# Outer products of a gated recurrence: from a broadcast through DRAM to masked matmuls on TensorE

## The chip, the cores and the metric

The kernel runs on one NeuronCore of a Trainium2 chip, in one launch. The metric is the device time of one execution in microseconds (us); less is better. Engines are named as in the profile: PE (TensorE) with its weight loads PEld, DVE (VectorE), ACT (ScalarE), POOL (GpSimd) and SP (SyncE, which only issues transfers here).

## What is computed

One decoder layer runs on 512 prompt tokens and, beside them, on one new token of each of 8 sample requests: a mixer of two head groups (a gated linear recurrence, HGRN2, and differential attention), memory cross-attention and a SwiGLU block. The sample's attention reads a paged cache of 4096 keys and values per request (64 MiB each).

The change is in the sample's recurrence. For each request b and each of 4 heads h, with a state S of 128 x 128:

```
S_new[b,h] = f[b,h][:, None] * S[b,h] + k[b,h][:, None] * v[b,h][None, :]
o[b,h]     = S_new[b,h].T @ q[b,h]
```

S_new is an output too (8 requests x 256 KB).

## The kernel before

**Staging.** The prompt's products are split in two fp32r parts (hi and lo for weights, sh and sl for activations), so each tile of a weight costs three PE matmuls of 128 x 512 (tiles `mm`). Weights stream from DRAM through `raw` tiles; ACT rounds them to `hi`, DVE forms the remainder `lo`, both at most HILO = 3 steps ahead of PE. The weight order is: input projection, memory keys and values (w_mk, w_mv), w_out, w_mq, w_mo, then the feed-forward chunks. The paged keys (`cache_k`) and then the values (`cache_v`) stream through six 512 KB buffers (`stream`, lines 934 to 940; KBUFS) on SP's queue while the prompt's products run; `score_keys` (line 991) makes the `ks` matmuls from them. SP issues a load when a buffer has come free.

**What sets the order.** Every piece of work is a generator, and a planner written in the kernel (`Weave`, line 312) picks, while the program is built, which generator goes on. It uses a clock of its own (`Clock`, line 134) with costs per instruction and per transfer (all transfers priced by bytes alone, line 257, in one line behind each other), and a rank per generator. So the order of instructions on each engine is fixed before the run, and each engine takes its instructions strictly in that order. The sample's recurrence has rank 4, the prompt's attention heads rank 3, the prompt's products rank 9 (they fill what is left). Tiles of PSUM are eight banks of 128 x 512 fp32; a generator asks for one (`at_room`) and gives it back (`at_give`), at most AT_MAX = 4 of the kind `at`.

**The recurrence** (`sample_recurrence`, line 1474). It starts when the input projection of the sample is done. skT holds the keys as [128 key components, head, request], sfT the gates, svq the values as [4 heads x 32 rows, 128], of which 8 rows per head are requests. svq is written to DRAM (`spill`, line 569, tile `vd`). Then for each request b in turn: POOL issues the load of the state (`st`, 256 KB, line 1492) and a load of that request's four value rows from DRAM to all 128 partitions (`load_row`, line 575: tile `kv`, 256 KB, line 1494); ACT scales the four heads of `kv` by the key column (line 1498), which makes the outer products in place; DVE masks the queries (`qm`) and makes st = f * st + kv, one instruction per head (line 1509); POOL issues the store of the new state (line 1513); PE makes the outputs (`so`, line 1517) and DVE adds them up in `ohg`. One request's transfers are issued only after the store of the one before.

**What follows.** The end of the recurrence (`S["hgo"]`, line 1533, after the transposition of `on`) is asked for at line 2152: if it is there before the third step of w_out's weights, the sample's half of the output projection is made from the weights as they pass for the prompt (lines 2153 to 2163), and four of eight extra loads of w_out (line 1879) drop out; otherwise all eight are loaded later.

All instructions are recorded through one helper, so the profile shows L305 for each; they are told apart by the names of their tiles.

Of the kernel before, what the change touches and what calls it, by code (L numbers as in the profile page):

```python
# [12 lines left out]
F32 = mybir.dt.float32  # L13
F32R = mybir.dt.float32r
I32 = mybir.dt.int32
AF = mybir.ActivationFunctionType
ALU = mybir.AluOpType
AX = mybir.AxisListType
PSUM = bass.MemoryType.PSUM

P = 128
# [4 lines left out]
NB = 8  # L26
HEADS = 4
# [351 lines left out]
def decode_step(ctx: ExitStack, tc: tile.TileContext, io: dict):  # L379
# [4 lines left out]
    act = clock.engine("act", real.scalar)  # L384
    dve = clock.engine("dve", real.vector)
    pool = clock.engine("pool", real.gpsimd)
# [8 lines left out]
    dp = ctx.enter_context(tc.tile_pool(name="dp", bufs=1, space=bass.MemoryType.DRAM))  # L395
    cnt = [0]

    def nm(s):
        cnt[0] += 1
        return f"{s}{cnt[0]}"  # L400

    def ring(p, shape, tag, bufs, name, dt=F32):
        return clock.alloc(tag, bufs, p.tile(list(shape), dt, tag=tag, bufs=bufs, name=nm(name)))

    def keep(shape, name):
        return cp.tile(list(shape), F32, name=name)


    def slot(s, shape=(P, T), dt=F32):
        return fp.tile(list(shape), dt, tag="slot", bufs=SLOTS, name=nm(s))  # L410
# [18 lines left out]
    def bank_counter(kind, most):  # L429
        banks[kind] = 0  # L430

        def room(n=1):
            fits = lambda: banks[kind] + n <= most and sum(banks.values()) + n <= 8
            yield fits
            yield clock.bank_free(n)
            while not fits():
                yield fits
            banks[kind] += n

        def give(n=1):  # L440
            banks[kind] -= n
            clock.release(kind, n)

        def tile(s=kind):
            return clock.bank(kind, ps.tile([P, T], F32, tag="ps", bufs=8, name=nm(s)))

        return room, give, tile

    mm_room, mm_give, mmt = bank_counter("mm", MM_MAX)
    at_room, at_give, att = bank_counter("at", AT_MAX)  # L450
# [5 lines left out]
    def small(shape, s="s", st="p", bufs=3):  # L456
        n = int(np.prod(shape[1:]))
        return ring(sp, shape, f"{st}{n}", bufs, s)
# [4 lines left out]
    def rsmall(shape, s):  # L463
        return small(shape, s, "r", 2)

    def quadt(s, shape=(P, P), tag="quad", bufs=4):
        return ring(sp, shape, tag, bufs, s)
# [4 lines left out]
    def mm(out, a, b, start, stop):  # L472
        pe.matmul(out, lhsT=a, rhs=b, start=start, stop=stop)

    def tr(out, a, i):
        pe.transpose(out, a, i)
# [17 lines left out]
    for n, shape in PARAMS:  # L494
        c = int(np.prod(shape))
# [9 lines left out]
    ident, ropes, cmask = views["ident"], views["ropes"], views["cmask"]  # L505
# [54 lines left out]
    def s_tr(q, use):  # L560

        yield from at_room()
        pt = att("str")
        tr(pt[:, :P], q, ident)
        yield (pt,)
        use(pt[:, :P].rearrange("p (g b) -> p g b", b=32))
        at_give()

    def spill(q, name):

        d = dp.tile([P, P], F32, name=name)
        pool.dma_start(d, q)
        return d.rearrange("(g b) c -> b g c", b=32)

    def load_row(dst, d, b):

        pool.dma_start(dst.rearrange("p (g c) -> p g c", g=4), d[b].partition_broadcast(P))


    sizes = [512] * (DFF // 512)  # L580
# [725 lines left out]
    def sigmoid(out, e, z):  # L1306

        act.activation(e, z, AF.Exp, scale=-1.0)
        yield
        dve.tensor_scalar(out, e, BIG, 1.0, op0=ALU.min, op1=ALU.add)  # L1310
        dve.reciprocal(out, out)
# [139 lines left out]
    def s_headnorm(o, use):  # L1451

        sq = quadt("hsq")
        s1 = rsmall([P, 1], "hs1")
        act.activation(sq, o, AF.Square, accum_out=s1)
        rs = rsmall([P, 1], "hrs")
        rstd_from(s1, rs, 1.0 / P)
        yield
        on = quadt("on")
        dve.tensor_scalar(on, o, rs, None, op0=ALU.mult)  # L1460
        yield
        yield from s_tr(on, use)
# [11 lines left out]
    def sample_recurrence(sqT, sfT, svq, sgT):  # L1474
        skT = keep([P, 4, 8], "skT")
        lb3 = lb.unsqueeze(2).to_broadcast([P, 4, 8])
        om3 = omlb.unsqueeze(2).to_broadcast([P, 4, 8])
        sig = rsmall([P, 4, 8], "sig")
        yield from sigmoid(sig, skT, sfT)
        dve.scalar_tensor_tensor(skT, skT, BIG, sig, op0=ALU.min, op1=ALU.mult)  # L1480
        dve.tensor_tensor(skT, skT, om3, op=ALU.mult)
        dve.tensor_tensor(sig, sig, om3, op=ALU.mult)
        dve.tensor_tensor(sfT, sig, lb3, op=ALU.add)
        yield
        sig2 = rsmall([P, 4, 8], "sig")
        yield from sigmoid(sig2, sig2, sgT)
        dve.tensor_mul(sgT, sgT, sig2)
        vd = spill(svq, "vd")
        yield from room(2)
        for b in range(NB):  # L1490
            st = slot("st")
            pool.dma_start(st, io["state"][b])
            kv = slot("kv")
            load_row(kv, vd, b)
            yield
            for h in range(HEADS):
                sl = slice(h * P, (h + 1) * P)
                act.activation(kv[:, sl], kv[:, sl], AF.Copy, scale=skT[:, h, b : b + 1])
            qm = quadt("qm", (P, 4, 32))
            dve.tensor_tensor(  # L1500
                qm,
                sqT[:, :, b : b + 1].to_broadcast([P, 4, 32]),
                ohrow[:, 7 - b : 39 - b].unsqueeze(1).to_broadcast([P, 4, 32]),
                op=ALU.mult,
            )
            yield
            for h in range(HEADS):
                sl = slice(h * P, (h + 1) * P)
                dve.scalar_tensor_tensor(
                    st[:, sl], st[:, sl], sfT[:, h, b : b + 1], kv[:, sl], op0=ALU.mult, op1=ALU.add  # L1510
                )
            yield
            pool.dma_start(io["hg_sample"][b], st)
            yield from at_room()
            po = att("so")
            for h in range(HEADS):
                mm(po[32 * h : 32 * h + 32, :P], qm[:, h, :], st[:, h * P : (h + 1) * P], True, True)
            yield (po,)
            if b == 0:
                dve.tensor_copy(ohg, po[:, :P])  # L1520
            else:
                dve.tensor_add(ohg, ohg, po[:, :P])
            at_give()
        give(2)
        yield
        pool.memset(mixT_s[:, :4, :], 0.0)
        yield from s_headnorm(
            ohg,
            lambda oht: dve.scalar_tensor_tensor(
                mixT_s[:, :4, :8], oht[:, :, :8], hgcol, sgT, op0=ALU.mult, op1=ALU.mult  # L1530
            ),
        )
        S["hgo"] = True
# [588 lines left out]
    def follower():  # L2122
# [8 lines left out]
        for i, c0 in enumerate(ORDER):  # L2131
# [11 lines left out]
            else:  # L2143
                S["v"] = keep([P, P], "vs")
                act.copy(S["v"], out)
                weave.add(store(io["v_sample"], S["v"]), 3)
        pv_give()
        weave.add(sample_recurrence(c[0], c[512], c[1024], c[1536]), 4, "ad")
        weave.add(sample_rest(), REST)
        done["seen"] += 16  # L2150
# [462 lines left out]
```

## Time and profile before

| | |
|---|---|
| time, median of 3 runs (lowest to highest) | 1142.68 us (1138.63 to 1144.46) |
| profiled execution: its own time | 1134.85 us |
| profiled execution: span from first to last instruction | 1133.1 us |
| mean granted clock of TensorE | 0.974 of full |
| DMA traffic | 279.75 MB, mean 247 GB/s |

Times of instructions are read from the profiled execution, whose own time is 1.75 us above its span. Stretches are given in us from the start of the span. The DMA share is the mean busy share of the core's 16 DMA engines. The queue q1 carries SP's and ACT's transfers, q0 those that POOL issues. The granted clock of TensorE is given as a share of full speed, 1.00 or 0.50, and a stretch that has both shows a value in between.

### The profile page before, as it was taken

The page shows a single profiled execution, that of the slowest core. Times are in us where ns is not written, and L with a number is a line of the kernel's source. Part 1 is how long each engine was busy: PE and PEld are TensorE (multiplying, and loading weights), DVE is VectorE, ACT ScalarE, POOL GpSimd, SP SyncE. Part 2 cuts the span into 40 slices and gives each one's busy share as a digit, 9 for nine tenths or more (in the row PEclk, how much of TensorE's full clock was granted, in tenths as well). Part 3 has the DMA queues.
Part 4 walks back from the last instruction along what each step waited for, and adds up shares of the span by engine and source line. Part 5 has one row for each costly group of instructions (what it writes and reads, how often), then busy time and mean ns, then how long its engine had stood idle before and what let it go on. Part 6 is the DMA issues. An engine that isn't in the chain of part 4 may idle for free.

```text
span 1133.1 us, 23098 instructions
## 1 busy us (share of the span) xinstructions
PE 1072.3 (95%) x8846; PEld 777.3 (69%) x8846; DVE 546.1 (48%) x1126; ACT 428.3 (38%) x915; POOL 70.4 (6%) x97
## 2 busy tenths in 40 slices
PE   8999799987987889899999999999999999999997
PEld 6777587865665557466666666776577677777776
DVE  6743777534654654444443443453343333443535
ACT  6413443436454556333444332341232221222333
POOL 0000010213101110000300000000000000000002
PEclk9999899988998989999999999999999999999999
DMA  7979665998999995999998799579978982234102
GB/s 255 352 242 324 206 215 174 291 253 259 319 308 278 274 304 169 309 329 332 319 338 285 241 325 343 201 244 359 344 266 291 351 305 75 63 89 129 38 1 75
DMA packets 143376, 279.75 MB, mean 247 GB/s; under 512 B 15281, under 2 KB 20529, under 8 KB 143266
## 3 DMA queue, kind: packets, MB, share of 16 engines
q1 hardware_dynamic: 137970, 264.13, 67.8%
q0 software_dynamic: 4064, 13.05, 6.1%
q8 instruction: 69, 1.13, 0.4%
q10 hardware_dynamic: 1232, 1.11, 0.3%
q14 instruction: 41, 0.34, 0.1%
HBM read 269.35 MB, written 8.88 MB: 246 GB/s over the span
## 4 chain that ended last, share of the span: by engine, by line
PE 81%; DMA 10%; DVE 3%; issue 3%; ACT 1%; SPq 1%; POOL 0%; DVEq 0%; POOLq 0%; ACTq 0%
PE mm L305 56%; DMA cache_k<-cache_k 6%; PE pv L305 5%; PE ks L305 4%; PE sgu L305 2%; PE cs L305 2%; PE sdn L305 1%; DMA kv<-vd 1%; PE ss L305 1%; PE co L305 1%; PE sgm L305 1%; PE pd L305 1%; PE sacc L305 1%; PE oda L305 1%; PE cpv L305 1%
## 5 line engine op out<-in xcount | busy, mean ns | idle before, releaser
L305 DVE TENSOR_TENSOR lo<-raw,hi 128x512 fp32r<-128x512 f32 (+1 forms) x260 | 176.6, 681 | 434.2 <-ACT hi L305 406.1
L305 PE MATMUL mm<-sh,hi 128*128 128x512 f32 (+1 forms) x832 | 339.8, 408 | 4.2 <-ACT sh L305 3.9
L305 ACT CAST hi<-raw 128x512 fp32r<-128x512 f32 (+1 forms) x260 | 157.5, 607 | 490.5 <-PE mm L305 443.3
L305 PE MATMUL mm<-sl,hi 128*128 128x512 f32 (+1 forms) x832 | 324.1, 390 | 0.8 <-DVE sl L305 0.8
L305 PE MATMUL mm<-sh,lo 128*128 128x512 f32 (+1 forms) x832 | 323.0, 388 | 0.0
L305 PEld LDWEIGHTS mm<-sh,hi 128*128 128x128 f32 x832 | 157.2, 189 | 78.6 <-issue 39.0
L305 PEld LDWEIGHTS mm<-sh,lo 128*128 128x128 f32 x832 | 157.5, 189 | 34.0 <-DVE lo L305 0.4
L305 PEld LDWEIGHTS mm<-sl,hi 128*128 128x128 f32 x832 | 157.8, 190 | 28.9 <-DVE sl L305 1.4
L305 PE MATMUL ks<-cache_k,qst 128*32 128x128 f32 x2048 | 72.3, 285 | 16.1 <-DMA cache_k<-cache_k 16.0
L305 PEld LDWEIGHTS ks<-cache_k,qst 128*32 128x32 f32 x2048 | 57.6, 114 | 32.7 <-DMA cache_k<-cache_k 24.0
L305 PE MATMUL pv<-cache_v,wt 128*32 128x512 f32 x512 | 63.4, 608 | 0.0
L305 PE MATMUL mm<-hi,sh 128*128 128x512 f32 x128 | 54.5, 426 | 0.0
L305 PE MATMUL mm<-lo,sh 128*128 128x512 f32 x128 | 50.5, 395 | 0.0
L305 PE MATMUL mm<-hi,sl 128*128 128x512 f32 x128 | 50.5, 394 | 0.0
L305 DVE TENSOR_TENSOR res<-mm,res 128x512 f32<-128x512 f32 (+1 forms) x68 | 42.2, 652 | 9.2 <-PE mm L305 9.2
L305 PEld LDWEIGHTS pv<-cache_v,wt 128*32 128x32 f32 x512 | 14.5, 110 | 31.1 <-issue 22.1
L305 DVE SCALAR_TENSOR_TENSOR lo<-raw,par,hi 128x512 fp32r<-128x512 f32 x16 | 13.2, 826 | 35.1 <-ACT hi L305 35.1
L305 PEld LDWEIGHTS mm<-hi,sh 128*128 128x128 f32 x128 | 24.3, 190 | 7.9 <-issue 3.1
L305 PE MATMUL mm<-hi,mh 128*128 128x512 f32 x64 | 28.5, 446 | 0.9 <-ACT hi L305 0.9
L305 PEld LDWEIGHTS mm<-hi,sl 128*128 128x128 f32 x128 | 24.3, 190 | 5.5
L305 PEld LDWEIGHTS mm<-lo,sh 128*128 128x128 f32 x128 | 24.4, 191 | 4.5 <-issue 0.5
L305 PE MATMUL mm<-lo,mh 128*128 128x512 f32 x64 | 25.2, 394 | 0.2 <-DVE lo L305 0.2
(419 smaller groups left out, 1210.3 us busy)
## 6 DMA issues: line engine op xcount, KB each, us to landing
cache_k<-cache_k SPq DMA_DIRECT2D x256, 256.0 KB, 5.6
cache_v<-cache_v SPq DMA_DIRECT2D x256, 256.0 KB, 4.8
raw<-w_in SPq DMA_DIRECT2D x27, 512.0 KB, 5.1
raw<-w_down SPq DMA_DIRECT2D x22, 512.0 KB, 4.2
raw<-w_gate SPq DMA_DIRECT2D x20, 512.0 KB, 5.0
raw<-w_up SPq DMA_DIRECT2D x20, 512.0 KB, 4.5
cache_mem_k<-cache_mem_k SPq DMA_DIRECT2D x16, 512.0 KB, 6.2
cache_mem_v<-cache_mem_v SPq DMA_DIRECT2D x16, 512.0 KB, 7.4
```

Of the source, the lines that this page charges most:

```text
L305: ins = getattr(self.engine, op)(*a, **k)
```

## The change

The values are no longer written to DRAM and read back. Once, ahead of the loop, the keys are copied to a zeroed tile with 32 columns per head (`padded`), transposed on PE to rows (`krows`: row 32 h + b is the key of head h and request b), the values are laid out as a block-diagonal tile (`vcols`: rows of head h hold their value in the columns of head h, zeros elsewhere), and a mask with a column per request is made from the identity (`mine`). For each request, DVE masks the key rows (`km`), and one fp32 matmul of 128 x 128 by 128 x 512 makes all four outer products in a PSUM bank (`kv`), from which DVE's st = f * st + kv reads. The four ACT instructions and the load of `kv` are gone; the bank is held until the four DVE instructions are done.

```diff
-    def spill(q, name):
-
-        d = dp.tile([P, P], F32, name=name)
-        pool.dma_start(d, q)
-        return d.rearrange("(g b) c -> b g c", b=32)
-
-    def load_row(dst, d, b):
-
-        pool.dma_start(dst.rearrange("p (g c) -> p g c", g=4), d[b].partition_broadcast(P))
...
         dve.tensor_mul(sgT, sgT, sig2)
-        vd = spill(svq, "vd")
         yield from room(2)
+
+        krows, vcols = quadt("krows", tag="rows", bufs=1), slot("vcols")
+        pool.memset(vcols, 0.0)
+        padded, mine = quadt("padded"), rsmall([P, 32], "mine")
+        dve.memset(padded, 0.0)
+        dve.tensor_copy(padded.rearrange("p (h b) -> p h b", h=4)[:, :, :NB], skT)
+        dve.tensor_reduce(mine, ident.rearrange("p (h b) -> p b h", h=4), axis=AX.X, op=ALU.add)
+        yield
+        yield from s_tr(padded, lambda pt: dve.tensor_copy(krows, pt.rearrange("p g b -> p (g b)")))
+        for h in range(HEADS):
+            r = slice(32 * h, 32 * h + 32)
+            act.copy(vcols[r, h * P : (h + 1) * P], svq[r])
+        yield
         for b in range(NB):
             st = slot("st")
             pool.dma_start(st, io["state"][b])
-            kv = slot("kv")
-            load_row(kv, vd, b)
-            yield
-            for h in range(HEADS):
-                sl = slice(h * P, (h + 1) * P)
-                act.activation(kv[:, sl], kv[:, sl], AF.Copy, scale=skT[:, h, b : b + 1])
+            km = quadt("km")
+            dve.tensor_scalar(km, krows, mine[:, b : b + 1], None, op0=ALU.mult)
             qm = quadt("qm", (P, 4, 32))
...
             yield
+            yield from at_room()
+            kv = att("kv")
+            mm(kv, km, vcols, True, True)
+            yield (kv, st)
             for h in range(HEADS):
                 sl = slice(h * P, (h + 1) * P)
                 dve.scalar_tensor_tensor(
                     st[:, sl], st[:, sl], sfT[:, h, b : b + 1], kv[:, sl], op0=ALU.mult, op1=ALU.add
                 )
+            at_give()
             yield
             pool.dma_start(io["hg_sample"][b], st)
```

## Rows read from the trace of the kernel before

**Rows 1.** Page: busy time of the engines over the span.

```profile
PE 1072.3 (95%) x8846; PEld 777.3 (69%) x8846; DVE 546.1 (48%) x1126; ACT 428.3 (38%) x915; POOL 70.4 (6%) x97
```

**Rows 2.** Stretches: busy us of PE, PEld, DVE, ACT, POOL; clock, DMA share, GB/s.

```profile
60.00:125.00 65.00, 65.00 (x905) 51.18 (x904) 28.17 (x58) 20.18 (x47) 0.54 (x1) 1.00 0.87 291
...
212.00:415.00 203.00, 172.49 (x1716) 124.45 (x1705) 103.82 (x259) 97.07 (x243) 34.61 (x48) 0.92 0.96 281
...
450.00:600.00 150.00, 146.90 (x839) 93.80 (x838) 65.73 (x116) 59.55 (x123) 10.77 (x9) 0.99 0.94 323
...
880.00:1134.00 254.00, 242.81 (x1571) 186.64 (x1569) 108.77 (x188) 69.47 (x136) 5.75 (x6) 0.98 0.38 123
```

**Rows 3.** PE's waits in 212 to 415: total us, times, longest.

```profile
PE ks L305 <- DMA cache_k<-cache_k: 16.0, 10, 6.0
PE sc L305 <- ACT pr L305: 4.9, 1, 4.9
PE so L305 <- issue: 3.6, 1, 3.6
PE pt L305 <- ACT pr L305: 2.3, 1, 2.3
```

**Rows 4.** Stretches of 5 us with a lowered clock, columns as in rows 2.

```profile
235.00:240.00 5.00, 5.00 (x34) 3.30 (x37) 1.98 (x6) 0.58 (x1) 1.82 (x3) 0.50 0.91 315
240.00:245.00 5.00, 5.00 (x66) 4.17 (x59) 0.69 (x1) 0.62 (x1) 0.00 (x0) 0.91 1.21 104
265.00:270.00 5.00, 4.96 (x23) 2.35 (x23) 0.00 (x0) 1.47 (x3) 0.00 (x0) 0.68 0.90 289
360.00:365.00 5.00, 4.93 (x41) 2.93 (x39) 0.30 (x1) 1.16 (x5) 0.00 (x0) 0.62 1.02 367
405.00:410.00 5.00, 5.00 (x42) 3.37 (x44) 2.92 (x9) 2.92 (x8) 0.00 (x0) 0.50 0.90 311
410.00:415.00 5.00, 5.00 (x61) 3.63 (x51) 2.27 (x8) 2.88 (x7) 2.93 (x7) 0.84 0.93 281
```

**Rows 5.** ACT in 395 to 407, in order of time: start, us, what, wait.

```profile
401.97 1.28 ACT L305 ACTIVATE kv<-kv,skT 128x128 f32<-128x128 f32 x4 [9.32 <-DMA kv<-vd]
```

**Rows 6.** DMA queues in 222 to 234: packets, MB, share.

```profile
q0 software_dynamic: 83, 0.27, 47.6%
q1 hardware_dynamic: 1021, 1.92, 43.6%
```

**Rows 7.** DMA in 212 to 415: queues; issues with median us to landing.

```profile
q1 hardware_dynamic: 26544, 48.07, 67.1%
q0 software_dynamic: 2651, 8.62, 28.6%
...
st<-state POOLq DMA_DIRECT2D x8, 256.0 KB, 6.1
...
kv<-vd POOLq DMA_DIRECT2D x8, 256.0 KB, 11.4
```

**Rows 8.** PE around a 128x512 fp32 matmul and a transposition, 425 to 428.

```profile
426.47 1.02 PE L305 MATMUL ss<-hq,ones 128*128 128x512 f32 x2
427.33 0.27 PE L305 MATMUL str<-con,on 128*128 128x128 f32 x1
427.36 0.47 PE L305 MATMUL mm<-sh,hi 128*128 128x512 f32 x1
427.67 0.39 PE L305 MATMUL mm<-sl,hi 128*128 128x512 f32 x1
427.90 0.40 PE L305 MATMUL mm<-sh,lo 128*128 128x512 f32 x1
```

**Rows 9.** Groups by tile (kv, S): ns min/median/max, starts, shapes.

```profile
L305 ACT ACTIVATE kv<-kv,skT x32: 384/387/412, 232.0 to 402.9; 128x128 f32<-128x128 f32 x32
...
L305 DVE SCALAR_TENSOR_TENSOR S<-S,bhg,pst x12: 347/348/349, 147.4 to 214.5; 128x128 f32<-128x128 f32 x12
```

**Rows 10.** SP's queue: longest wait in 212 to 415.

```profile
SPq L305 <- PE ks L305: 18.6, 16, 4.6
```

## The prediction

> **What bounds the kernel now.** I read the page's busy times first: PE is busy for 95% of the span [rows 1], so over the whole kernel PE sets the pace, and a change elsewhere pays only where PE waits or runs at its lower clock. Next the stretches [rows 2]. The recurrence lies in 212 to 415. There PE is busy for 172.5 of 203.0 us, so 30.5 us are idle, the mean granted clock is 0.92, and the DMA engines are busy for 0.96 of the time. Compare two stretches that stream the same kinds of weights and cache pages: 60 to 125, with a DMA share of 0.87 and PE never idle, and 450 to 600, with 0.94 and 3.1 us idle in 150. So PE keeps up below about 0.9 and begins to lose above it; in 212 to 415 it is the transfers that are late.
>
> The waits of PE say whom it waits for [rows 3]: 16.0 us for pages of the cached keys, 4.9 and 2.3 us (sc, pt) for ACT, 3.6 us at a `so` matmul, 26.8 us together. The ACT waits come from the recurrence itself: ACT stands 9.3 us at the first `kv` scaling until the broadcast lands [rows 5], everything behind it in ACT's order stands too, and PE stops for 4.9 us. The `so` matmul comes behind the same chain. After the longer waits the clock falls to the 1.2 GHz level: with PE's busy time times one minus the granted clock, the six stretches [rows 4] cost 2.5 + 0.45 + 1.6 + 1.9 + 2.5 + 0.8 = 9.7 us.
>
> Why are the transfers late? In 222 to 234 the only transfer on POOL's queue is one `kv` broadcast: 0.27 MB take 47.6% of 12 us, 5.7 us of all 16 engines, while 1.92 MB on the other queue take 5.2 us [rows 6]. Over 212 to 415, q1 moves 48.07 MB in 67.1% of 203 us, 2.83 us per MB [rows 7]. POOL's queue has 8.62 MB in 28.6%, 58.1 us; its 6.52 MB that are not `kv` cost 18.5 us at q1's rate, which leaves 39.6 us for eight broadcasts, 5.0 each. That agrees with the 5.7 measured alone. **The broadcast takes a fifth of the stage's DMA time for a twenty-seventh of its bytes.**
>
> A rule speaks against this reading. The Trainium skill, "DMA: Bandwidth & Descriptors", section Specifications, gives 512 bytes as the least transfer for line rate, and a row of `kv` is made of 512-byte pieces: by it a broadcast would cost what its bytes cost and the change would free next to nothing. The trace disagrees (5.7 us for 0.27 MB), and I follow the trace; what would follow from the rule is the second rival.
>
> **The change, part by part.**
>
> Removed, DMA: eight broadcasts, 39.6 us of engine time (the 64 KB spill adds too little to count). The stage's DMA time was 0.96 x 203 = 194.9 us; 155.3 remain.
>
> Removed, ACT: 32 scalings of 0.387 us [rows 9], 12.4 us, and the waits ahead of them. Four small copies come instead, under 0.4 us each by the same row. ACT was busy for 97 of 203 us [rows 2], so the work was hidden; what counts is that nothing on ACT now stands behind a transfer of the recurrence.
>
> Removed, POOL: nine transfer issues; one fill of a tile is added. POOL is busy for 34.6 of 203 us: nothing, either way. The state's load and the store are issued in the same places as before.
>
> Added, PE: eight fp32 matmuls of 128x512. One such matmul (two records) took 427.33 - 426.47 = 0.86 us, and the first prompt matmul behind such a change of form started its successor after 0.31 instead of 0.23 us [rows 8]. So 8 x (0.86 + 0.08) = 7.5, and one transposition, at most 0.27: 7.8 us. PE is the engine that sets the end, so all of it counts, at full clock; at the lower level it would be up to twice that, at least 0 if it falls into a wait.
>
> Added, DVE: eight maskings of the key rows and a handful of small ones ahead of the loop, at most 0.35 us each by a three-operand instruction of 128x128 [rows 9]: under 5 us on an engine busy for 104 of 203 us. Reading `kv` from PSUM costs nothing more: that row is an instruction with a PSUM operand, and at 348 ns it has the price of the recurrence's own, which read SBUF. If DVE's cover were gone, the sum would be 5 us worse.
>
> Added, waits: `kv` needs DVE's masking and a PSUM bank, and st = f * st + kv needs the matmul and the state's load. Behind that DVE instruction stand the remainders of the weights, behind the `so` matmul the whole of PE. The state lands 6.1 us after its issue, the broadcast landed after 11.4 [rows 7], and the order of the work had room for the latter in most rounds; I take 0 for this wait, and price it as a rival. The bank is held for some 3 us a round, with prompt matmuls to run meanwhile: 0.
>
> Moved: the planner's order. Its own clock knows neither the price of the broadcast nor this stage's waits, so the places of the `so` matmuls change little; but the recurrence ends a few us earlier in it, and the transposition that ends it at 427.33 stands between the output projection's first matmuls [rows 8], right where line 2152 decides. It may fall the other way: then narrow matmuls move forward and four loads of 512 KB drop out, 2.1 MB or 5.9 us of DMA time in stretches where PE hardly waits. I take 0; what a new order can do later is bounded by the 11.2 idle us of the last stretch [rows 2], either way.
>
> **The sum.** 155.3 us of DMA for PE work of 172.5 - 9.7 + 7.8 = 170.6 us is a share of 0.91, between the two comparison stretches. I leave the idle rate of the fuller one, 3.1 / 150 x 203 = 4.2 us, to the cache: 16.0 - 4.2 = 11.8 gained. The ACT waits go (7.2), the `so` wait goes (3.6): 22.6 of 26.8. The lowered clock goes in proportion: 9.7 x 22.6 / 26.8 = 8.2. With 7.8 added: 22.6 + 8.2 - 7.8 = 23.0 us less. The profiled execution took 1134.85 us, 7.8 below the median of the runs, 1142.68; I carry the difference over and predict 1142.68 - 23.0 = 1119.7, **1120 us**. Bounds: all waits and all clock regained, 36.5 - 7.8 = 28.7 less, 1114; with the later idle time on top, 1103; without DVE's cover, with waits of 5 us left and some of the idle time added, 1130.
>
> **The rivals.**
>
> *Buffers, not bandwidth.* SP issues a page only when PE frees a buffer, and its queue waited 18.6 us for that [rows 10]. If this rather than the rate makes the pages late, the 16.0 us and their clock stay. Gained are 10.8 us of waits and the clock behind those two, 2.95 + 3.3 [rows 4]; less 7.8, that is 9.2: 1133.5. Against it: the same six buffers left no wait in 60 to 125.
>
> *The broadcast is not what fills the engines*, as the rule above would have it. Then 2.1 MB at 2.83 us per MB, 5.9 us, are saved, the stage stays at a share of 0.96, and 6 us are gained at most, with the new PE work inside the waits that remain: 1137 to 1143, no change that can be told.
>
> *A wait on the state takes the place of the wait on the values; slower.* PE takes the outer product, then `so`, in order, and a late state stops both. One such stop cost 3.65 us and 2.95 of clock [rows 3, 4], 6.6 together. The change wins 36.5 - 7.8 = 28.7 without it, so from the fifth round of eight on it is slower; in all eight rounds 52.8 stand against 28.7, 1167. Against it: the state has a 5 us shorter way than the values had [rows 7], and PE stopped so in one round of eight even then.
>
> *Given back later.* The new order loses in the last stretches what this one gains, up to the 11.2 us there and more: around 1140.
>
> **How the numbers follow.** A measurement of this kernel can tell about 0.5%, 5.7 us, from no change. Chances: the forecast 0.67 (its own range 1105 to 1131), buffers 0.12, the broadcast not at fault 0.07, slower by the state 0.08, given back 0.06. Faster by over 0.5% (under 1137.0): the forecast and most of the buffers' case, 0.77. Within: the second rival, most of the last and a rest, 0.13. Slower: 0.10. The range runs from the upper gain, 1103, to the buffers' case and a little above, 1136.
>
> **What would show it.** Right: in the recurrence's stretch, shorter by some 20 us, POOL's queue takes under a tenth of the DMA time; PE's waits on cache pages fall to about 4 us; no wait of PE behind ACT over 2 us; eight `kv` matmuls of about 0.9 us; stretches at 0.50 to 0.68 clock nearly gone. Wrong: DMA share still 0.95 with fewer bytes per us (the second rival), SP's queue waiting for `ks` while pages are late (the first), DVE or PE waiting for `st` (the third), a PE wait after 880 that was not there (the fourth).

## The result, and the profile after

The changed kernel takes 1108.6 us (median of 4 runs, 1105.32 to 1109.8) against 1140.66 us (1133.83 to 1144.46) in the runs beside them: ratio 0.9726, 95% interval 0.9683 to 0.9769, 32 us less. The forecast was 1120, 23 us less; the time lies in its range and the direction is right, but the gain is 1.4 times the forecast. The profiled execution took 1109.8 us, 25 us less than that of before, which was itself 6 us below its median.

Page of the changed kernel, busy times, as [rows 1]:

```profile
span 1108.0 us, 23125 instructions
PE 1066.2 (96%) x8863; PEld 774.3 (70%) x8863; DVE 550.3 (50%) x1140; ACT 420.9 (38%) x887; POOL 63.0 (6%) x89
```

Stretches of the changed kernel, columns as in [rows 2]; 212 to 390 is the recurrence, and 390 to 425 is what comes next:

```profile
212.00:390.00 178.00, 171.46 (x1845) 126.23 (x1843) 115.89 (x298) 100.72 (x251) 25.20 (x35) 1.00 0.92 322
390.00:425.00 35.00, 30.57 (x152) 19.18 (x153) 11.61 (x26) 14.77 (x28) 5.32 (x10) 0.95 0.60 209
```

The idle time of PE in the recurrence's stretch fell from 30.5 us of 203 to 6.5 of 178, and the granted clock is 1.00 where the mean was 0.92 [rows 2]. The waits of PE in that stretch, which answer to [rows 3]:

```profile
PE ks L305 <- DMA cache_k<-cache_k: 3.3, 6, 1.2
PE oda L305 <- ACT pr L305: 1.3, 1, 1.3
```

The pages come on time (3.3 us of waits for 16.0), and the waits behind ACT's `kv` and at `so` are gone. The queues in 212 to 390 and the state's load, as [rows 7]:

```profile
q1 hardware_dynamic: 27827, 50.34, 81.7%
q0 software_dynamic: 2042, 6.65, 9.6%
...
st<-state POOLq DMA_DIRECT2D x8, 256.0 KB, 6.5
```

POOL's queue takes 17.1 us of DMA time (9.6% of 178) for 58.1 before. The new work, from the groups on the tile `kv` (two records to a matmul, as in [rows 8]):

```profile
L305 DVE SCALAR_TENSOR_TENSOR st<-st,scols,kv x32: 333/340/347, 236.7 to 367.1; 128x128 f32<-128x128 f32 x32
...
L305 PE MATMUL kv<-vcols,km x16: 592/593/697, 235.5 to 363.0; 128*128 128x512 f32 x16
```

DVE's instruction takes 340 ns with `kv` in PSUM, as priced. One thing went another way than I had set it: the planner's branch. The weights of the output projection are now used as they pass, in the middle of the prompt's output projection:

```profile
L305 PE MATMUL sgm<-raw,mixT_s x32: 378/379/403, 400.0 to 441.1; 128*32 128x256 f32 x32
L305 PE MATMUL sgm<-w_out,mixT_s x32: 378/379/404, 703.7 to 705.3; 128*32 128x256 f32 x32
```

In the kernel before all 64 records were `sgm<-w_out`, at 725 to 735 us. The first `pv` matmul came at 446.7 us before and comes at 407.7 now, 39 us earlier; the first `cq` of the query projection came at 527.7 and comes at 505.7, only 22 us earlier. Something between the two gives time back, 17 us by these two marks; the run without the branch, below, shows 7.5 us of the whole.

### The profile page after: what moved, and what is told of

It reads as the page before. It is cut to its first block, busy times and chain, and to the rows that moved or that the text cites. A ratio compares the mean times of both kernels' runs of the same rounds, so it can differ in the third digit from the quotient of the medians.

```text
span 1108.0 us, 23125 instructions
## 1 busy us (share of the span) xinstructions
PE 1066.2 (96%) x8863; PEld 774.3 (70%) x8863; DVE 550.3 (50%) x1140; ACT 420.9 (38%) x887; POOL 63.0 (6%) x89
## 4 chain that ended last, share of the span: by engine, by line
PE 87%; DMA 4%; DVE 4%; issue 2%; ACT 2%; SPq 1%; DVEq 0%; ACTq 0%
PE mm L305 61%; PE pv L305 5%; PE ks L305 5%; PE sgu L305 2%; DMA cache_k<-cache_k 2%; PE cs L305 2%; PE sdn L305 1%; PE sgm L305 1%; PE co L305 1%; PE ss L305 1%; SPq L305 1%; DMA cache_v<-cache_v 1%; PE pd L305 1%; PE sacc L305 1%; PE oda L305 1%
## 5 line engine op out<-in xcount | busy, mean ns | idle before, releaser
L305 PE MATMUL pv<-cache_v,wt 128*32 128x512 f32 x512 | 67.1, 599 | 3.2 <-DMA cache_v<-cache_v 3.2
L305 PE MATMUL ks<-cache_k,qst 128*32 128x128 f32 x2048 | 64.9, 274 | 3.3 <-DMA cache_k<-cache_k 3.3
L305 PEld LDWEIGHTS ks<-cache_k,qst 128*32 128x32 f32 x2048 | 54.5, 110 | 16.9 <-issue 8.6
```

The lines of the kernel that those rows point to most:

```text
L305: ins = getattr(self.engine, op)(*a, **k)
```

## The experiments

The kernels built on the kernel before keep its order of instructions on PE, DVE and ACT exactly, and so do the unused broadcasts and the repeated matmuls for the changed kernel: what is added there is issued past the planner's clock, or priced in it as what it replaces. So a difference is due to the edit and not to a new order. Only the run without following has another order, which is what it is about.

**The price of the broadcast: an ordinary load in its place.**

```diff
-            load_row(kv, vd, b)
+            pool.dma_start(kv, io["state"][b])
```

> The kernel before, with the order of every engine's work unchanged, but each request's kv tile is filled by an ordinary load of the same 256 KB (128 rows of 2 KB of a state) in place of the broadcast of four value rows; so the outer products, and with them the sample's recurrence, are not computed from the values. Theory (the broadcast's way of moving the bytes is what is paid): POOL's queue falls from 58 to under 30 us of DMA time in 212 to 415, the kv wait of ACT is gone, PE's waits on cache pages fall from 16.0 to 3 to 6 us, and the time falls by 25 to 33 us, ratio to the kernel before 0.971 to 0.979; no PE work is added here, so it may be a little below the changed kernel. Rival (a broadcast costs what its bytes cost): nothing changes, ratio 0.997 to 1.003, and the changed kernel's gain has to come from ACT or from the new order.

Measured: 1095.1 us, ratio 0.9623 (0.9599 to 0.9647), 45 us less, beyond both expectations and below the changed kernel. Its queues in 212 to 400 and the waits of PE in 212 to 420:

```profile
q1 hardware_dynamic: 28972, 52.54, 79.1%
q0 software_dynamic: 3521, 11.45, 16.2%
...
kv<-state POOLq DMA_DIRECT2D x8, 256.0 KB, 7.5
```

```profile
PE sc L305 <- ACT pr L305: 1.5, 1, 1.5
PE ks L305 <- DMA cache_k<-cache_k: 0.7, 3, 0.3
```

The same bytes, the same order and the same ACT work, and the waits are gone: 11.45 MB on POOL's queue now cost 16.2% of 188 us, 2.7 us per MB, about the rate of the other queue (2.8). The rival by which a broadcast costs what its bytes cost has fallen. The recurrence's stretch of this run, columns as in [rows 2]:

```profile
212.00:380.00 168.00, 163.30 (x1772) 121.39 (x1774) 107.28 (x265) 100.00 (x252) 33.81 (x49) 1.00 0.97 344
```

The DMA engines are as busy as before (0.97, before 0.96 [rows 2]), and PE hardly waits for pages (0.7 us). What changed is what they move in that time: 344 GB/s for 281. So a high busy share does not by itself show that transfers come late.

**ACT's wait alone.** The broadcasts go to a tile that nobody reads, ACT scales a constant.

```diff
-            load_row(kv, vd, b)
+            load_row(rest, vd, b)
...
-                act.activation(kv[:, sl], kv[:, sl], AF.Copy, scale=skT[:, h, b : b + 1])
+                act.activation(kv[:, sl], fixed[:, sl], AF.Copy, scale=skT[:, h, b : b + 1])
```

> The kernel before with the same order of work and the same broadcasts, but they go to a tile that nobody reads, and ACT scales a constant tile in place of the values, so ACT never waits for a broadcast; the outer products are not the reference's. It takes the head-of-line wait away and leaves the DMA load. My theory (both count, the DMA load more): the ACT waits of PE (7.2 us), the so wait (3.6) and their clock (6.3) go, up to 17 us, part of it turns into longer waits on cache pages: 6 to 14 us less, ratio 0.988 to 0.995. Rival 1 (all through ACT): ratio 0.971 to 0.980. Rival 2 (all through the late pages): ratio 0.996 to 1.003.

Measured: 1132.5 us, ratio 0.9946 (0.991 to 0.9981). The waits of PE, 212 to 420:

```profile
PE ks L305 <- DMA cache_k<-cache_k: 20.5, 16, 5.2
```

As expected: PE's waits behind ACT end and reappear in part as waits for pages, 20.5 us for 16.0 (the profiled execution, 1124.6 us, is the fastest of ten). With the transfers left as dear as they were, ACT's place behind the broadcast is worth some 6 us, 2 to 10 by the interval. If the two parts simply add up, which was not tried, the rest of the 45 us is transfer time.

**The changed kernel again, with the broadcasts back in, unused.** First the changed kernel itself, as the measure for this run and the next two.

> The changed kernel once more, as the measure for the three runs beside it: ratio to the kernel before 0.968 to 0.977.

Measured: 1106.7 us, ratio 0.9742 (0.9681 to 0.9804).

```diff
             km = quadt("km")
+            real.gpsimd.dma_start(
+                spare[0].rearrange("p (g c) -> p g c", g=4),
+                vd.rearrange("(g b) c -> b g c", b=32)[b].partition_broadcast(P),
+            )
```

> The changed kernel with its order of work, but the values are spilled and broadcast again, eight times 256 KB to a tile that nobody reads. No engine waits for them. If the DMA time of the broadcasts is the main cost: the share of POOL's queue goes back up by about 40 us of DMA time, waits on cache pages come back (3.3 us to 12 to 20, with 3 to 6 us of lowered clock), and the time rises by 12 to 22 us over the changed kernel, ratio to the kernel before 0.979 to 0.990. Rival (the gain came from ACT's waits and the new order): within 3 us of the changed kernel, ratio as there.

Measured: 1149.9 us, ratio 1.0103 (1.0042 to 1.0165), 43.2 us above the changed kernel: twice what I expected, and as much as the plain load had won. No engine reads what these transfers bring; only POOL, which issues them, waited 7.9 us in all, for the spill and for one of them. The waits of PE, 212 to 420, and the stretch:

```profile
PE ks L305 <- DMA cache_k<-cache_k: 25.1, 17, 6.1
```

```profile
212.00:415.00 203.00, 174.41 (x1740) 123.31 (x1730) 105.74 (x275) 90.36 (x224) 30.40 (x41) 0.92 0.93 276
```

Two tests in two orders of work, one taking the broadcasts' price out and one putting it in, agree on 43 to 45 us for eight transfers of 256 KB. The clock is back at 0.92 with them, and the DMA share of 0.93 is lower than the 0.97 of the plain load, where PE hardly waited.

**The price of the matmuls.** Each outer product is made three times.

```diff
+            for _ in range(2):
+                real.tensor.matmul(kv, lhsT=km, rhs=vcols, start=True, stop=True)
             mm(kv, km, vcols, True, True)
```

> The changed kernel with its order of work, but each outer product is made three times in a row into the same bank. If PE's time sets the end in this stretch, 16 more matmuls of 0.86 us cost 13.8 us, and half of that, 6.9, is the price of the eight in the changed kernel; the time rises by 10 to 15 us, ratio to the kernel before 0.981 to 0.986. Rival (the matmuls fall into waits that are there anyway): under 5 us.

Measured: 1120.8 us, ratio 0.9859 (0.9802 to 0.9916), 14.0 us more for 16 matmuls, 0.88 each. By that the eight of the changed kernel cost 7.0; I had 0.86 each, 6.9. The 0.9 us that I had added for the change of form and the transposition is not tested by this run.

**The branch in the planner's order.**

```diff
-        if "hgo" in S:
+        if False:
```

> The changed kernel, but the sample's half of the output projection is not taken from the weights as they pass: all eight extra loads of w_out come back, 2.1 MB more, and the order of work after the recurrence is that of the other branch. My prediction priced this at nothing: within 4 us of the changed kernel, ratio to the kernel before 0.968 to 0.980. Rival (the branch was a good part of the gain): 6 us or more slower than the changed kernel.

Measured: 1099.2 us, ratio 0.9663 (0.9607 to 0.9718), 7.5 us less than the changed kernel: the branch that I had set to nothing costs time, on the side that neither of the two expectations named. One place where it may go is seen on POOL's queue. In the changed kernel, POOL in 360 to 420:

```profile
406.64 0.54 POOL L305 DMA_DIRECT2D out_mem_v<-mv  x1 [24.76 <-ACT mv L305]
407.17 3.71 POOL L305 DMA_DIRECT2D res<-xpT  x7
```

and with the branch off:

```profile
378.33 3.19 POOL L305 DMA_DIRECT2D res<-xpT  x6
...
403.52 1.12 POOL L305 DMA_DIRECT2D out_mem_v<-mv  x2 [19.84 <-ACT mv L305]
```

In the new order a store that waits 24.8 us for ACT stands ahead of the eight loads of the residual, 2.1 MB. They start at 407 and meet the first pages of the values. DMA issues in 405 to 425 of the changed kernel, and PE there (in 407 to 426):

```profile
cache_v<-cache_v SPq DMA_DIRECT2D x13, 256.0 KB, 9.0
res<-xpT POOLq DMA_DIRECT2D x8, 256.0 KB, 9.5
```

```profile
416.25 1.05 PE L305 MATMUL pv<-cache_v,wt 128*32 128x512 f32 x2 [0.65 <-DMA cache_v<-cache_v]
418.29 1.04 PE L305 MATMUL pv<-cache_v,wt 128*32 128x512 f32 x2 [1.00 <-DMA cache_v<-cache_v]
420.10 1.05 PE L305 MATMUL pv<-cache_v,wt 128*32 128x512 f32 x2 [0.77 <-DMA cache_v<-cache_v]
```

With the branch off a page lands after 5.5 us in 402 to 422, and PE is busy for all of 404 to 494. That the collision is the cause is read from the two traces; it was not tried by itself, and the wait rows hold 3.2 of the 7.5 us. The rest is not settled: between the profiled executions of the changed kernel beside this run (1105.4 us) and of this run (1097.0 us), PE's idle time falls by 4.0 us and its busy time by 4.4.

**What makes the broadcast dear.** Four layouts of its source, and a control, all on the kernel before in its own order of work.

Pieces of 512 bytes, each read once, from four states:

> As the plain load, same order of work, but the 256 KB are fetched in pieces of 512 bytes, four per partition, each read once from four different states; the recurrence is again not computed from the values. It splits the cause of the broadcast's price. If the size of the pieces is at fault: as the kernel before, 4 to 6 us of DMA time per load and ratio 0.995 to 1.003. If it is that 128 partitions read the same rows: as the plain load, about 1 us per load (0.74 by its bytes) and ratio 0.971 to 0.980. I hold the second for likelier, 0.65 to 0.35.

Measured: 1097.3 us, ratio 0.963 (0.9594 to 0.9667): cheap. POOL's queue in 212 to 400:

```profile
q0 software_dynamic: 3492, 11.36, 16.3%
```

That is 2.7 us per MB, as in the plain load. Small pieces by themselves are not at fault. This run shows one thing more, which I used only at the end: the four pieces of a partition lie 512 KB apart here, in every other state, so a round pitch by itself is cheap too, as long as no other partition reads the same pieces.

One shared row of 2 KB:

```diff
-        d = dp.tile([P, P], F32, name=name)
-        pool.dma_start(d, q)
-        return d.rearrange("(g b) c -> b g c", b=32)
+        d = dp.tile([32, 4, P], F32, name=name)
+        for g in range(4):
+            pool.dma_start(d[:, g, :], q[32 * g : 32 * g + 32, :])
+        return d
```

> The kernel before with the same order of work and the full computation, but the values are written to DRAM with the four heads of a request side by side, so each partition's part of the broadcast is one row of 2 KB and not four pieces of 512 bytes. If the size of the pieces is at fault, this is as cheap as the plain load, ratio 0.971 to 0.980, and a cheap remedy. If the shared source is at fault, the price stays at 4 to 6 us of DMA time per broadcast and the ratio at 0.99 to 1.003. Three more short stores go ahead of the loop, 64 KB in all as before.

Measured: 1100.0 us, ratio 0.9663 (0.9637 to 0.9688): cheap too. In 223 to 230 of it, one `kv` is the only transfer of POOL's queue:

```profile
q0 software_dynamic: 83, 0.27, 12.7%
...
kv<-vd POOLq DMA_DIRECT2D x1, 256.0 KB, 3.5
```

0.9 us of DMA time (12.7% of 7) for the same 83 packets that took 5.7 us before [rows 6]. Reading one row from 128 partitions is not at fault by itself either. So I had two clean halves and neither was the cause; left were the pitch of 16 KB between the four pieces, and small pieces together with sharing.

The four pieces 640 bytes apart:

```diff
+        d = dp.tile([32, 4, 160], F32, name=name)[:, :, :P]
```

> The kernel before with the same order of work and the full computation; the four heads of a request lie near each other in DRAM but not in one row: 512 bytes each, 640 bytes apart, so the broadcast is again made of pieces of 512 bytes that all partitions share. The plain load in pieces was cheap, and so was the broadcast of one row of 2 KB, so neither the size of the pieces nor the sharing alone is at fault. Left are the pitch of 16 KB between the four pieces of the kernel before, and small pieces together with sharing. If the pitch: about 1 us of DMA time per broadcast, ratio 0.963 to 0.972. If small shared pieces: 4 to 6 us per broadcast, ratio 0.99 to 1.003. I give the pitch 0.6.

Measured: 1096.5 us, ratio 0.9632 (0.9587 to 0.9678).

The four pieces 16.5 KB apart:

```diff
+        d = dp.tile([4, 33, P], F32, name=name)[:, :32]
```

> The kernel before with the same order of work and the full computation; the values lie as before, with the four heads far apart, but at a pitch of 16.5 KB in place of 16 KB. If it is the round pitch that is slow, this is cheap, 1 us per broadcast and ratio 0.963 to 0.972. If it is the distance, or small shared pieces at any distance, it stays as before, 4 to 6 us and ratio 0.99 to 1.003. With the run beside it this gives three outcomes: both cheap (the round pitch), only the near one cheap (the distance), both dear (small shared pieces).

Measured: 1098.6 us, ratio 0.9661 (0.9609 to 0.9714). Both cheap. One broadcast of the second in 222 to 231, the only load that POOL issued there:

```profile
q0 software_dynamic: 92, 0.29, 15.7%
```

That is 1.4 us of DMA time for all that POOL's queue moved in these 9 us. These layouts are spilled by four short stores, the kernel before by one; the control has the four stores and the old pitch:

```diff
-        d = dp.tile([4, 33, P], F32, name=name)[:, :32]
+        d = dp.tile([4, 32, P], F32, name=name)
```

> The control for the three layouts: the kernel before with the same order of work, the values spilled by four short stores as in those runs, but laid out at the pitch of 16 KB that they have in the kernel before. If the pitch is what is slow, the four stores change nothing: 4 to 6 us of DMA time per broadcast and ratio 0.99 to 1.005. If it was the one store that made the broadcast slow, by where it puts the rows, this is cheap too, ratio 0.963 to 0.972.

Measured: 1142.2 us, ratio 1.0036 (0.9993 to 1.0078), and 50.4% of 11 us, 5.5 us, for one broadcast in 223 to 234:

```profile
q0 software_dynamic: 80, 0.26, 50.4%
```

So the cause is the pitch of a shared source: the four rows that all 128 partitions read lie 16 KB apart, and 512 bytes more between them take 40 us off the kernel. Both parts belong to it, since unshared pieces 512 KB apart were cheap and so were shared ones at the two other pitches. No other round pitch was tried with a shared source, so whether 16 KB or roundness in general is what counts stays open.

**The version that beats both.** The row broadcast in the order of the kernel before, each one issued one request ahead, the outer products on ACT as before:

```diff
+        ahead = send(0)
         for b in range(NB):
             st = slot("st")
             pool.dma_start(st, io["state"][b])
-            kv = slot("kv")
-            load_row(kv, vd, b)
+            kv, ahead = ahead, send(b + 1) if b + 1 < NB else None
```

> The version that may beat both: the kernel before with its order of work, the broadcast of one row of 2 KB, and each broadcast issued one request earlier, so that ACT does not wait for it. The full computation. In the row broadcast alone ACT waited 7.5 us for the values and PE 1.8 us behind ACT. I expect no wait of ACT on the values and 2 to 5 us less than the row broadcast alone, which is the time of the plain load: 1094 to 1099 us, ratio 0.960 to 0.966. Rival (nothing is left to gain there): ratio 0.966 to 0.969 as the row broadcast alone.

Measured: 1092.2 us (median of 6 runs, 1090.86 to 1095.98), ratio 0.9607 (0.9575 to 0.9639). That is below both intervals of the changed kernel, 14 to 16 us faster, with all of the computation and no work added to PE. ACT's wait on `kv` fell from 7.5 to 2.6 us, not to none as I had expected. Against the row broadcast alone the intervals just overlap, and so they do against the changed kernel without the branch (0.9663, 0.9607 to 0.9718). So the lead over the changed kernel is in part the branch of the planner, and not only where the outer products are made.

## Why the prediction was right, and where it was off

*What bounds the stretch: right in what PE waits for, wrong in the sign.* PE lost time there to late transfers and to ACT behind a broadcast, and it got it back: waits for pages 3.3 us where I had left 4.2, no wait behind ACT over 1.3 us, the clock at 1.00, POOL's queue at 9.6% of the stretch. But I read the overload from the DMA share, with a bound at about 0.9 from two stretches. The plain load has 0.97 and waits of 0.7 us; the unused broadcasts have 0.93 and waits of 25.1 us. The share says that the engines have something to do, not that it is late. What told of the price was the time per MB of each queue.

*The broadcast's engine time as the price: right, and the rule set against it was set aside rightly for this kernel, though not for the reason I gave.* The Trainium skill, "DMA: Bandwidth & Descriptors", section Specifications, asks for pieces of at least 512 bytes, and the run with pieces read once agrees with it: they take 2.7 us per MB, as the plain load does. I had read the rows as a price of broadcasting, and they were a price of four shared rows that lie 16 KB apart.

*The size of the removal: the term that was mis-sized.* I forecast 22.6 us of waits and 8.2 of clock, 30.8. Two experiments measured it: 45.0 taken out of the kernel before, 43.2 put into the changed one. In the profiled executions of the kernel before and the plain load it is 39.7 (1134.85 to 1095.2). The page of the plain load, as [rows 1]:

```profile
span 1093.4 us, 23098 instructions
PE 1059.9 (97%) x8846; PEld 772.7 (71%) x8846; DVE 545.4 (50%) x1126; ACT 428.3 (39%) x915; POOL 68.9 (6%) x97
```

PE's idle time fell from 60.8 to 33.5 us, by 27.3, and its busy time, in which the lowered clock shows, by 12.4. So the two sums that I held back belonged to the change: 4.2 us for pages that stay late, taken from the DMA share, and 1.5 us of the clock, by proportion. With them I would have had 36.5; the other 3 us are nearly all busy time beyond the 9.7 that I had from six stretches. The remaining 5 us lie between the execution I summed over and the median: the kernel before ran from 1126.94 to 1146.43 us over all the runs made of it, and I carried only the difference of the medians over, as if the gain did not depend on it. That a slower execution loses more to the broadcasts is how I read this; no run shows it.

*The matmuls: right.* 0.86 us each forecast, 0.88 measured by repetition.

*The planner's order at nothing: wrong.* The prediction named the place and the branch, and that it might fall the other way; it looked at the four loads that drop out, and not at what the changed order does to the loads behind a store on POOL's queue. The branch costs 7.5 us; that the order of POOL's transfers is the reason is argued from the traces, for 3.2 of them.

The terms as measured close: 45.0 gained, 7.0 and 7.5 paid, 30.5 net, against 30.8 (1137.56 to 1106.74) between kernels measured beside each other and 32.1 in the first runs. Each term has an interval of several us, so that they meet so closely is partly chance. There is luck in the forecast too: the removal was 14 us too small and the branch 7.5 us too cheap, and the two errors work against each other.

*The rivals.* Buffers instead of bandwidth: SP had the same six buffers in the plain load and its queue still waited for them, in 212 to 380,

```profile
SPq L305 <- PE ks L305: 16.6, 16, 3.1
```

for 18.6 us before [rows 10], while PE's waits for pages fell to 0.7 us; out. The broadcast not at fault: out by the plain load. A wait on the state: the only waits of DVE at the new instruction were 3.8 us for the matmul, none for the state; out. Given back later: not where the rival put it, since PE is idle for 10.1 us from 855 to the end and was for 11.2 in the last stretch before [rows 2]; but the new order does lose the 7.5 us of the branch.

## What to carry to other kernels

Before an expensive transfer is replaced by arithmetic, ask what makes it expensive: engine time per byte against that of the other queue shows that it is dear, and changing its layout, its sharing and its pieces one at a time shows why. Here some 40 us hung on the pitch of four shared rows, and the repair that leaves the work where it was costs the engine that sets the end nothing, where the one that moves it there pays 7 us. A high busy share of the DMA engines does not say that transfers are late; the waits for them and the bytes moved per us do. And where a program's order is planned ahead, a shorter step can flip a decision elsewhere: the order that follows, and what then stands behind the first waiting instruction on each queue, belongs in the sum.

## What the runs showed of the hardware that was not expected

Reading four rows of 512 bytes at a pitch of 16 KB from all 128 partitions takes 5.5 to 5.7 us of all 16 DMA engines for 256 KB. At a pitch of 640 bytes, of 16.5 KB, or as one row of 2 KB, the kernel takes 1096.5 to 1100.0 us, close to the 1095.1 with an ordinary load; one broadcast of the row took 0.9 us, one at 16.5 KB at most 1.4. Pieces of 512 bytes that lie 512 KB apart and are each read once take 2.7 us per MB, as an ordinary load. The Trainium skill, "DMA: Bandwidth & Descriptors", section Latency and other measured facts, tells of slow copies where the row pitch in DRAM is a large power of two, 2 to 8 MiB in its figures, and of padding as the remedy. The runs here show the like at 16 KB for a shared source, and that 512 bytes of padding suffice. Whether the four rows share a part of the memory was not tried.

Eight such transfers that nobody reads lengthen the kernel by 43.2 us. And the DMA engines can be busy for 0.97 of a stretch (344 GB/s) with 0.7 us of waits for them, or for 0.93 (276 GB/s) with 25.1.
